# Three raw tiles of the down weights, two tiles for unrounded MLP units and one buffer for the plain quarters' parts, in a two-layer decoder trunk

## The chip, the cores and the metric

One core of one Trainium2 chip runs the whole program. The metric is device time in microseconds (us) of one launch; the time of a kernel is the median of several runs. A profile is taken of one further execution. The engines are TensorE (PE in the profile; PEld is its weight load), VectorE (DVE), ScalarE (ACT), GpSimd (POOL) and SyncE (SP); SP and POOL issue the DMAs that matter here.

## The reference

The kernel computes a trunk of two layers for 256 tokens of width 2048, in float32:

```
for l in range(2):
    h = rmsnorm(x, attn_norm_g[l]);  proj = h @ w_in[l]      # q | k | v | gate_b | gate_c | conv_in
    attn = differential attention of 8 heads (normed q and k, relative bias, subtracted softmaxes)
    conv = gate_b * causal_conv3(gate_c * conv_in)
    x = x + concat([attn, conv]) @ w_out[l]
    hm = rmsnorm(x, mlp_norm_g[l]) @ w_up[l]                 # 2048 -> 8192
    x = x + square(relu(hm)) @ w_down[l]                     # 8192 -> 2048
```

The change touches only the last two lines, the MLP.

## The kernel before

**Products.** TensorE works on float32 values that are rounded to a form it takes at full speed (F32R). So each operand is split into a high part (a rounded copy, made by ScalarE) and a low part (the value minus the high part, made by VectorE), and each product is three matmuls: high by high, high by low, low by high (TERMS, L48). What comes from weights goes raw by DMA into SBUF and is split there. For every 128x1024 stretch of weights this is one ScalarE copy of 1.06 us and one VectorE subtraction of 1.2 us.

**Up stage** (the loop at L999). The 8192 hidden units are made in 32 units of 256 (NP; i counts them). For each, two columns of up weights are multiplied (`up_part`, matmuls at L952, weights split at L818 and L819), evicted from PSUM (`evict`, ScalarE copy L962, VectorE add L963 into a tile `h`), and squared (`square`: relu L969, a factor per token L971, square L973, four sums L977 to L980). Then h is split into the parts of a tile f (L984, L985). Units of the list SEVEN are written unrounded to DRAM (L982); the others, but for the last two, as their two parts (L987).

Between the columns of unit i come the products of unit i − 2 (LAG) with the first 1024 columns of the down weights. A product of 2x2 blocks is done with seven block products in place of eight; so sums of the four quarters of the weights are wanted as well as the quarters themselves. `quarters` (L834) makes three jobs for a unit: `plain` loads the raw tile ("draw", L829, tag "draw" of the pool dpool) and splits one quarter into b1h and b1l, two into b2h and b2l (through `parts`, ScalarE L842, VectorE L843); `sums` makes the sums t (L856, L859, L860) and t13h, t13l; `more` makes t24h, t24l. The matmuls of the seven products stand at L995. The last two units, 30 and 31, have no sums and are multiplied in the ordinary way, eight block products each (`ordinary`, L1069, matmuls at L1077), after VectorE and ScalarE have begun to add the seven products into x (`seven_onto`, L1052, L1058, L1066).

**Down stage**, for the other 1024 columns. It begins with units 30 and 31 against whole columns (L1152). Then units 0 to 25 (27 in the second layer) are read back from DRAM, one unit ahead. `pair` (L1090 on) does this: a unit that is not in SEVEN comes back as its parts (tile "fb", L1097); a unit of SEVEN (2, 4, 7, 9 and so on) comes back unrounded into a tile "back" (L1101), which has the tag "h" and so shares the buffers of the up stage's h, and is split again (ScalarE L1102, VectorE L1103). Units of SEVEN are multiplied with `quarters` again, the others in the ordinary way. Blocks of four columns finish the stage.

**Order.** TensorE has its order written out by hand (`manual_schedule`). All weights pass one list of jobs (`Weights`); `take` hands the next to TensorE and has made the jobs up to three ahead of it (AHEAD). ScalarE, VectorE, POOL and SP are given their order by a scheduler, when the kernel is built; it places an instruction by its estimates once its inputs and its buffer are free, so an instruction of a later part of the program can come before one of an earlier part. Only instructions passed to `late` (L124) are kept in the order of the program. On the chip each engine then runs its instructions in that fixed order.

**Pools** (sizes for each partition): upool holds four raw tiles of 8 KB, fpool the tile h (4 KB, one buffer) and f (8 KB, two), dpool two raw tiles "draw" (8 KB), spool the quarters' parts: b1h and b1l (2 KB) and b2h and b2l (4 KB) with two buffers each, t, t13 and t24 with one.

Of the kernel before, what the change touches and what calls it, by code (L numbers as in the profile page):

```python
# [9 lines left out]
F32 = mybir.dt.float32  # L10
# [5 lines left out]
P = 128  # L16
# [12 lines left out]
CH = 512  # L29
# [76 lines left out]
def trunk(ctx: ExitStack, tc: tile.TileContext, x, w_in, w_out, conv_w, q_norm_g, k_norm_g,  # L106
# [19 lines left out]
    def bank(name):  # L126
        return ps.tile([P, CH], F32, tag="bank", name=name)
# [662 lines left out]
    def mlp(l, mnorm, last):  # L790
# [5 lines left out]
        with ExitStack() as scope:  # L796
            upool = scope.enter_context(tc.tile_pool(name="upool", bufs=4))
            fpool = scope.enter_context(tc.tile_pool(name="fpool", bufs=2))
            dpool = scope.enter_context(tc.tile_pool(name="dpool", bufs=2))
            spool = scope.enter_context(tc.tile_pool(name="spool", bufs=1))  # L800
            work.start(mnorm.factors(), 1)

# [2 lines left out]
            raws, forms = {}, {}  # L805
# [20 lines left out]
            def load_rows(i, col, pool=dpool, tag="draw"):  # L826
                raw = pool.tile([P, 2, 2 * CH], F32, tag=tag, name=tag)
                for k in range(2):
                    nc.sync.dma_start(  # L829
                        raw[:, k], w_down[l][(i * 2 + k) * P:(i * 2 + k + 1) * P,  # L830
                                             col:col + 2 * CH])
                return raw

            def quarters(i, col=0):  # L834


                keep = late if i == 0 or (i == SEVEN[0] and col) else lambda ins: None

                def parts(src, tag, bufs):
                    hi = spool.tile(list(src.shape), F32R, tag=f"{tag}h", name=f"{tag}h", bufs=bufs)  # L840
                    lo = spool.tile(list(src.shape), F32R, tag=f"{tag}l", name=f"{tag}l", bufs=bufs)
                    keep(nc.scalar.activation(hi, src, AF.Copy))  # L842
                    keep(nc.vector.tensor_sub(lo, src, hi.bitcast(F32)))  # L843
                    return hi, lo

                def plain():
                    raw = forms["raw"] = load_rows(i, col).rearrange("p k (n c) -> p k n c", n=2)
                    h1, l1 = parts(raw[:, 0, 0], "b1", 2)
                    h2, l2 = parts(raw[:, 1], "b2", 2)
                    return (h1, l1), (h2[:, 0], l2[:, 0]), (h2[:, 1], l2[:, 1])  # L850

                def sums():
                    raw = forms["raw"]
                    t = forms["t"] = spool.tile([P, 4, CH], F32, tag="t", name="t")

                    keep(nc.vector.tensor_sub(t[:, 0:2], raw[:, :, 1], raw[:, 0]))  # L856
                    h, lw = parts(t[:, 0:2], "t13", 1)

                    keep(nc.vector.tensor_add(t[:, 2], t[:, 1], raw[:, 0, 0]))  # L859
                    keep(nc.vector.tensor_sub(t[:, 3], raw[:, 1, 0], t[:, 2]))  # L860
                    return (h[:, 0], lw[:, 0]), (h[:, 1], lw[:, 1])

                def more():
                    h, lw = parts(forms["t"][:, 2:4], "t24", 1)
                    return (h[:, 0], lw[:, 0]), (h[:, 1], lw[:, 1])

                if (i, col) == (0, 0):
                    made = {}
                    forms["plain"] = lambda: made.update(p=plain())
                    forms["sums"] = lambda: made.update(s=sums())  # L870
                    return lambda: made["p"], lambda: made["s"], more
                return plain, sums, more
# [65 lines left out]
            def column_bank():  # L938
                acc = ps.tile([P, CH], F32, tag="av", name="upc", bufs=1)
                return acc.rearrange("p (h s) -> p h s", h=2)  # L940

            def up_part(acc, kh):

                hi, lo = weights.take()
                for part, wt in ((0, hi), (1, lo)):
                    for k in range(8):
                        a = mT[kh * 2 + k // KG]
                        while not a.ready:  # L950
                            work.tick()
                        nc.tensor.matmul(  # L952
                            acc[:, 0] if part else acc, wt[:, k],
                            a.ap[:, 0, k % KG] if part else a.ap[:, :, k % KG],
                            start=(part == 0 and kh == 0 and k == 0),
                            stop=(part == 1 and kh == 1 and k == 7), skip_group_check=True)
                        if k % 4 == 3:
                            work.tick()

            def evict(acc, dst):  # L960
                ev = nat.tile([P, 2, S], F32, tag="wide", name="ev")
                nc.scalar.activation(ev, acc, AF.Copy)  # L962
                nc.vector.tensor_add(dst.rearrange("p a c -> p (a c)"), ev[:, 0], ev[:, 1])  # L963
# [28 lines left out]
            def product(n, f, a, b, start, stop):  # L992

                for m, (pa, pw) in enumerate(TERMS):
                    nc.tensor.matmul(prods[n], f[:, pa, a], b[pw],  # L995
                                     start=(start and m == 0), stop=(stop and m == 2))

            fs = {}
            for i in range(NP):  # L999
                j = i - LAG  # L1000
                end = i == NP - 1
                h = fpool.tile([P, 8, P], F32, tag="h", name="h", bufs=1)
                if i == 0:
                    two = mm.tile([P, 2, CH], F32, tag="mm2", name="up0")
                    two = [two[:, c].rearrange("p (h s) -> p h s", h=2) for c in range(2)]
                    for kh in range(2):
                        for c in range(2):
                            up_part(two[c], kh)
                    forms["plain"]()
                    for c in range(2):  # L1010
                        evict(two[c], h[:, 2 * c:2 * c + 2])
                    fs[0] = square(0, h)
                    forms["sums"]()
                    continue
                for c in range(2):
                    if i < LAG:
                        acc = bank("upw").rearrange("p (h s) -> p h s", h=2)
                    else:
                        acc = column_bank()
                    up_part(acc, 0)  # L1020
                    up_part(acc, 1)
                    evict(acc, h[:, 2 * c:2 * c + 2])
                    if c == 1:
                        fs[i] = square(i, h)
                    if j == 0 and c == 0:
                        for pair in ((1, 6), (2, 3)):
                            w2 = mm.tile([P, 2, CH], F32, tag="mm2", name=f"pr{l}{pair[0]}")
                            prods[pair[0]], prods[pair[1]] = w2[:, 0], w2[:, 1]
                        for n in (5, 7, 4):
                            prods[n] = bank(f"pr{l}{n}")  # L1030
                    if j >= 0 and c == 0:
                        b11, b21, b22 = weights.take()
                        t1, t3 = weights.take()
                        f = fs[j]
                        product(1, f, A11, b11, j == 0, end)
                        product(2, f, A12, b21, j == 0, False)
                        product(3, f, S4, b22, j == 0, False)
                        product(5, f, S1, t1, j == 0, end)
                        work.tick()
                    elif j >= 0:  # L1040
                        t2, t4 = weights.take()
                        f = fs[j]
                        product(7, f, S3, t3, j == 0, end)
                        product(6, f, S2, t2, j == 0, end)
                        product(4, f, A22, t4, j == 0, False)
                        work.tick()
# [45 lines left out]
            def pair(i, f=None, at=0):  # L1092

                if f is None:
                    f = apool.tile([P, 2, 8, P], F32R, tag="a", name="fb")
                if i not in SEVEN:
                    nc.gpsimd.dma_start(  # L1097
                        f[:, :, at:at + 4].rearrange("p a k c -> p a (k c)"), hid[i])
                    return f
                back = fpool.tile([P, 8, P], F32, tag="h", name="back", bufs=1)  # L1100
                nc.gpsimd.dma_start(back.rearrange("p a c -> p (a c)"), hid7[i])  # L1101
                nc.scalar.activation(f[:, 0], back, AF.Copy)  # L1102
                nc.vector.tensor_sub(f[:, 1], back, f[:, 0].bitcast(F32))  # L1103
                return f
# [154 lines left out]
```

## Time and profile before

| What | Value |
| --- | --- |
| Median of 3 runs | 2139.8 us (2139.35 to 2141.16) |
| The profiled execution | 2141.08 us |
| Its span, first to last instruction | 2139.3 us |
| Mean granted TensorE clock | 1.000 |

The page of the profile gives busy times of the engines, the chain of work that ended last, and groups of instructions; the trace behind it gives each instruction's start and duration, the idle time before it and the instruction that ended that idle time. A row of the timeline has start, duration (us), engine, line, operation, the tiles it writes and reads, shape and count; in brackets stands the idle time of the engine before it and what it waited for. Rows with a count over 1 are several like instructions in a row, and the duration is that of all. A matmul of 128x512 is drawn 0.39 us long, but the next one starts 0.23 us after it; durations of neighbours overlap also on VectorE and ScalarE.

### The profile page before, as it was taken

What the parts mean: (1) busy time and instruction counts of PE and PEld (TensorE: products, weight loads), DVE (VectorE), ACT (ScalarE), POOL (GpSimd) and SP (SyncE); (2) the same over time, 40 slices, a digit from 0 to 9 for tenths busy, and PEclk for the clock granted to TensorE, in tenths of its full rate; (3) what the DMA queues carried; (4) which work ended last, traced back from release to release, by engine and by line L of the source; (5) the groups of instructions that cost most, each with busy time, mean ns of one, the idle gap of its engine ahead of it and who ended that gap; (6) DMA issues with size and microseconds to landing.
All of it is one profiled execution on the core that took longest, in us unless ns stands there. A gap on an engine that the chain in (4) does not pass through costs nothing.

```text
span 2139.3 us, 29295 instructions
## 1 busy us (share of the span) xinstructions
PE 2130.0 (100%) x10925; PEld 1817.7 (85%) x10925; DVE 1700.6 (79%) x2316; ACT 1317.1 (62%) x1776; POOL 164.4 (8%) x226
## 2 busy tenths in 40 slices
PE   9999999999999999999999999999999999999999
PEld 8888888888888888888888888888888888888887
DVE  6778655798888888798766786557988888888986
ACT  6666445666666666565565765456666666665653
POOL 3110200000000000011111101000000000000110
PEclk9999999999999999999999999999999999999999
DMA  8555766577777777789656558656877777777983
GB/s 271 178 164 168 253 188 186 187 247 228 230 236 227 233 233 226 239 302 307 226 168 178 165 161 264 187 177 200 250 231 223 241 231 223 240 226 251 315 309 128
DMA packets 298254, 476.01 MB, mean 223 GB/s; under 512 B 12707, under 2 KB 193781, under 8 KB 298112
## 3 DMA queue, kind: packets, MB, share of 16 engines
q1 hardware_dynamic: 269120, 406.76, 60.8%
q0 software_dynamic: 28800, 67.24, 9.3%
q8 instruction: 85, 1.39, 0.3%
q14 instruction: 57, 0.47, 0.1%
q10 hardware_dynamic: 192, 0.15, 0.0%
HBM read 440.52 MB, written 33.58 MB: 222 GB/s over the span
## 4 chain that ended last, share of the span: by engine, by line
PE 97%; DVE 1%; ACT 1%; DMA 1%; issue 0%; DVEq 0%; ACTq 0%
PE upc L952 31%; PE pr L995 13%; PE dn L1077 8%; PE o L386 8%; PE gb L408 4%; PE k L386 4%; PE q L386 4%; PE v L386 4%; PE ci L408 4%; PE gc L408 4%; PE dn L995 2%; PE dn L1152 2%; PE pr1r L995 1%; PE pr0r L995 1%; PE upw L952 1%; PE up L952 1%
## 5 line engine op out<-in xcount | busy, mean ns | idle before, releaser
L303 DVE TENSOR_TENSOR wlo<-raw,whi 128x1024 fp32r<-128x1024 f32 x274 | 341.6, 1248 | 222.6 <-ACT whi L302 221.2
L302 ACT ACTIVATE whi<-raw 128x1024 fp32r<-128x1024 f32 x274 | 290.4, 1060 | 306.5 <-PE o L386 73.6
L952 PE MATMUL upc<-nT,uhi 128*128 128x512 f32 x1920 | 477.8, 391 | 1.1 <-ACT ev L962 1.1
L818 ACT ACTIVATE uhi<-uraw 128x1024 fp32r<-128x1024 f32 x256 | 271.3, 1061 | 283.3 <-PE upc L952 262.5
L952 PEld LDWEIGHTS upc<-nT,uhi 128*128 128x128 f32 x1920 | 352.6, 188 | 70.0 <-ACT ev L962 1.9
L819 DVE TENSOR_TENSOR ulo<-uraw,uhi 128x1024 fp32r<-128x1024 f32 x256 | 312.6, 1222 | 111.1 <-ACT uhi L818 107.3
L952 PEld LDWEIGHTS upc<-nT,ulo 128*128 128x128 f32 x1920 | 261.9, 190 | 18.7
L952 PE MATMUL upc<-nT,ulo 128*128 128x256 f32 x1920 | 267.7, 282 | 0.0
L1077 PE MATMUL dn<-whi,fb 128*128 128x512 f32 x528 | 166.1, 389 | 0.0
L386 PE MATMUL o<-whi,cat 128*128 128x512 f32 x512 | 159.5, 390 | 0.0
L302 ACT ACTIVATE whi<-uraw 128x1024 fp32r<-128x1024 f32 x66 | 70.1, 1062 | 87.4 <-PE dn L1077 79.3
L1077 PEld LDWEIGHTS dn<-whi,fb 128*128 128x128 f32 x528 | 99.1, 188 | 20.5
L386 PEld LDWEIGHTS o<-whi,cat 128*128 128x128 f32 x512 | 96.2, 188 | 19.7
L842 ACT ACTIVATE b2h<-draw 128x1024 fp32r<-128x1024 f32 x81 | 85.7, 1059 | 29.8 <-PE pr L995 22.0
L843 DVE TENSOR_TENSOR t13l<-t,t13h 128x1024 fp32r<-128x1024 f32 x81 | 99.2, 1224 | 6.1 <-ACT t13h L842 3.7
L1077 PE MATMUL dn<-wlo,fb 128*128 128x512 f32 x264 | 102.7, 389 | 0.0
L843 DVE TENSOR_TENSOR b2l<-draw,b2h 128x1024 fp32r<-128x1024 f32 x81 | 98.6, 1218 | 3.2 <-ACT b2h L842 3.2
L843 DVE TENSOR_TENSOR t24l<-t,t24h 128x1024 fp32r<-128x1024 f32 x81 | 98.8, 1219 | 1.5 <-ACT t24h L842 0.3
L386 PE MATMUL o<-wlo,cat 128*128 128x512 f32 x256 | 99.6, 389 | 0.0
L856 DVE TENSOR_TENSOR t<-draw 128x1024 f32<-128x1024 f32 x81 | 98.7, 1219 | 0.5
L303 DVE TENSOR_TENSOR wlo<-uraw,whi 128x1024 fp32r<-128x1024 f32 x66 | 80.5, 1222 | 21.7 <-ACT whi L302 15.3
L995 PE MATMUL pr<-t13h,f 128*128 128x512 f32 x240 | 93.8, 391 | 0.0
(408 smaller groups left out, 4111.3 us busy)
## 6 DMA issues: line engine op xcount, KB each, us to landing
uraw<-in_w_up_dram SPq DMA_DIRECT2D x128, 1024.0 KB, 6.5
raw<-in_w_in_dram SPq DMA_DIRECT2D x191, 512.0 KB, 3.9
draw<-in_w_down_dram SPq DMA_DIRECT2D x170, 512.0 KB, 4.6
uraw<-in_w_down_dram SPq DMA_DIRECT2D x66, 512.0 KB, 5.1
raw<-in_w_out_dram SPq DMA_DIRECT2D x64, 512.0 KB, 3.6
hid0p<-f POOLq DMA_DIRECT2D x20, 512.0 KB, 6.6
raw<-in_w_down_dram SPq DMA_DIRECT2D x10, 1024.0 KB, 5.1
fb<-hid0p POOLq DMA_DIRECT2D x20, 512.0 KB, 6.7
```

Source lines behind the costliest of these rows:

```text
L302: pair = (nc.scalar.activation(hi, raw, AF.Copy), nc.vector.tensor_sub(lo, raw, hi.bitcast(F32)))
L303: nc.vector.tensor_sub(lo, raw, hi.bitcast(F32)))
L386: nc.tensor.matmul(acc[:, t], a.ap[:, pa, k % KG, t * P:(t + 1) * P], (hi, lo)[pw][:, j], start=(k == 0 and n == 0), stop=(k == nk - 1 and ...
L408: nc.tensor.matmul(acc[:, f, 0] if part else acc[:, f], wt[:, k % 4, fs], a.ap[:, 0, k % KG] if part else a.ap[:, :, k % KG], start=(part ...
L818: pair = (nc.scalar.activation(hi, src, AF.Copy), nc.vector.tensor_sub(lo, src, hi.bitcast(F32)))
L819: nc.vector.tensor_sub(lo, src, hi.bitcast(F32)))
L842: keep(nc.scalar.activation(hi, src, AF.Copy))
L843: keep(nc.vector.tensor_sub(lo, src, hi.bitcast(F32)))
L856: keep(nc.vector.tensor_sub(t[:, 0:2], raw[:, :, 1], raw[:, 0]))
L952: nc.tensor.matmul(acc[:, 0] if part else acc, wt[:, k], a.ap[:, 0, k % KG] if part else a.ap[:, :, k % KG], start=(part == 0 and kh == 0 ...
L995: nc.tensor.matmul(prods[n], f[:, pa, a], b[pw], start=(start and m == 0), stop=(stop and m == 2))
L1077: nc.tensor.matmul(prods[p], f[:, pa, 2 * k + t], b[pw][:, n], start=(p in starts and k == 0 and m == 0), stop=(stop and k == 1 and m == 2))
```

## The change

Three buffer counts are changed. The plain quarters' parts (b1h, b1l, b2h, b2l) have one buffer where they had two, which frees 12 KB of each partition. In this room go a third raw tile "draw" of the down weights (8 KB) and a second tile of the tag "h" (4 KB), for h in the up stage and for back in the down stage. Beside that, the raw tile and the sums are kept in a dictionary of each unit's own (`mine`) in place of the shared one (`forms`); this alone changes no instruction. TensorE's instructions and their order stay the same. The order of ScalarE, VectorE, POOL and SP is worked out anew by the scheduler. Line numbers of the changed kernel are higher by two from L840 on.

```diff
-            dpool = scope.enter_context(tc.tile_pool(name="dpool", bufs=2))
+            dpool = scope.enter_context(tc.tile_pool(name="dpool", bufs=3))
...
+                mine = {}
+
                 def parts(src, tag, bufs):
...
                 def plain():
-                    raw = forms["raw"] = load_rows(i, col).rearrange("p k (n c) -> p k n c", n=2)
-                    h1, l1 = parts(raw[:, 0, 0], "b1", 2)
-                    h2, l2 = parts(raw[:, 1], "b2", 2)
+                    raw = mine["raw"] = load_rows(i, col).rearrange("p k (n c) -> p k n c", n=2)
+                    h1, l1 = parts(raw[:, 0, 0], "b1", 1)
+                    h2, l2 = parts(raw[:, 1], "b2", 1)
                     return (h1, l1), (h2[:, 0], l2[:, 0]), (h2[:, 1], l2[:, 1])
 
                 def sums():
-                    raw = forms["raw"]
-                    t = forms["t"] = spool.tile([P, 4, CH], F32, tag="t", name="t")
+                    raw = mine["raw"]
+                    t = mine["t"] = spool.tile([P, 4, CH], F32, tag="t", name="t")
...
                 def more():
-                    h, lw = parts(forms["t"][:, 2:4], "t24", 1)
+                    h, lw = parts(mine["t"][:, 2:4], "t24", 1)
...
-                h = fpool.tile([P, 8, P], F32, tag="h", name="h", bufs=1)
+                h = fpool.tile([P, 8, P], F32, tag="h", name="h", bufs=2)
...
-                back = fpool.tile([P, 8, P], F32, tag="h", name="back", bufs=1)
+                back = fpool.tile([P, 8, P], F32, tag="h", name="back", bufs=2)
```

## The prediction

> **What bounds the kernel now.** I read the head of the page and its shares of busy time first, then the sums of the chain of waits.
>
> ```profile
> span 2139.3 us, 29295 instructions
> PE 2130.0 (100%) x10925; PEld 1817.7 (85%) x10925; DVE 1700.6 (79%) x2316; ACT 1317.1 (62%) x1776; POOL 164.4 (8%) x226
> PE 97%; DVE 1%; ACT 1%; DMA 1%; issue 0%; DVEq 0%; ACTq 0%
> ```
>
> TensorE is busy 2130.0 of 2139.3 us and is 97% of the chain that ended last. All its idle time is 9.3 us (0.4%); nothing that leaves TensorE's work as it is can win more, and the change leaves it so: its instruction order is the same in both kernels. So I ask two things only: which of the 9.3 us go, and whether a new wait comes. Next, the waits of TensorE, the two lines that stand in the MLP (waited for, us in total, times, longest):
>
> ```profile
> PE upc L952 <- ACT ev L962: 1.1, 1, 1.1
> PE pr L995 <- DVE f L985: 0.9, 2, 0.5
> ```
>
> Then the windows, one in the steady up stage (columns: us, PE, PEld, DVE, ACT, POOL busy with counts, granted clock, DMA share, GB/s):
>
> ```profile
> 530.00:694.00 164.00, 164.00 (x880) 141.93 (x879) 145.73 (x197) 109.82 (x135) 6.24 (x10) 1.00 0.74 230
> ```
>
> There TensorE has no gap at all, while VectorE is busy 145.73/164.00 = 89%. It keeps up, but an instruction that comes at the wrong place in its row is followed by others without a hole to catch up in. That is what I look for below.
>
> **What the change takes away.** Three stalls in each layer's MLP, or two and a trace, read from the timeline of ScalarE and TensorE (start, us, engine, line, operation; in brackets the idle time before and what ended it).
>
> ```profile
> 430.20 0.63 ACT L842 ACTIVATE b1h<-draw 128x512 fp32r<-128x512 f32 x1 [2.69 <-DMA draw<-in_w_down_dram]
> 431.68 0.58 ACT L962 ACTIVATE ev<-upc 128x512 f32<-128x512 f32 x1
> 430.80 0.39 PE L995 MATMUL pr<-t24h,f 128*128 128x512 f32 x1
> 432.31 0.96 PE L952 MATMUL upc<-nT,uhi 128*128 128x512 f32 x3 [1.13 <-ACT ev L962]
> ...
> 470.11 0.40 PE L995 MATMUL pr<-b1l,f 128*128 128x512 f32 x1
> 470.97 0.50 PE L995 MATMUL pr<-b1h,f 128*128 128x512 f32 x1 [0.47 <-DVE f L985]
> ...
> 911.34 0.61 PE L1152 MATMUL dn<-whi,f 128*128 128x512 f32 x2
> 912.02 0.50 PE L1152 MATMUL dn<-wlo,f 128*128 128x512 f32 x1
> ...
> 1973.53 0.61 PE L1152 MATMUL dn<-whi,f 128*128 128x512 f32 x2
> 1974.21 0.50 PE L1152 MATMUL dn<-wlo,f 128*128 128x512 f32 x1
> ...
> 895.25 0.39 PE L1077 MATMUL pr<-whi,f 128*128 128x512 f32 x1
> 900.46 0.61 PE L1077 MATMUL pr<-whi,f 128*128 128x512 f32 x2
> ```
>
> From 895.25 to 900.46 are 23 matmuls without a stall, 5.21/23 = 0.227 us from start to start; what a start is later than that is a stall.
>
> (1) 432.31 − 430.80 − 0.23 = 1.28 us, first layer only: ScalarE stands 2.69 us at b1h until its raw tile has landed, and the eviction of upc, which could have run, stands behind it. A third raw tile lets that load go a pair earlier: gone. (2) 470.97 − 470.11 − 0.23 = 0.63 us, and by the waits' "0.9, 2" once more in the other layer: the low half of f is late because the one unrounded tile h is held. With a second h the chain of the next pair starts at once: gone, 1.26 us. (3) 912.02 − 911.34 − 2 × 0.227 = 0.23 us, and 1974.21 − 1973.53 − 2 × 0.227 = 0.23 in the other layer, a low part of the first columns of the down stage; VectorE's order there is rearranged, and I let it go in both layers: 0.46 us. Sum **−3.0 us** at most. Each restart also shows a slower first matmul (0.50 for 0.39), five times 0.11 = 0.55 in all, which I leave to the range.
>
> **What costs nothing: one b1 and one b2.** No instruction is added. In the order of the changed kernel these parts are written, as before, right behind the product that frees them; the trace of before already shows such a write waiting for the product:
>
> ```profile
> 616.28 1.06 ACT L842 ACTIVATE b2h<-draw 128x1024 fp32r<-128x1024 f32 x1 [0.43 <-PE pr L995]
> 629.94 0.40 PE L995 MATMUL pr<-b1h,f 128*128 128x512 f32 x1
> ```
>
> The next product that reads such a part starts 629.94 − 616.28 = 13.66 us after that write began. All four parts take some 3.6 us (the b1h row 0.63, b2h 1.06, and their low parts, by the 128x512 and 128x1024 subtracts shown below, 0.68 + 1.23). So TensorE's other matmuls hide it; without that cover it would be up to 3.6 us for each of some 30 quartered units a layer, and the cover would have to shrink by 10 us first. In the down stage it is thinner: at least one ordinary unit of 24 matmuls (24 × 0.227 = 5.4 us) stands between two quartered ones, beside the rest of the quartered unit's own matmuls. Still over 3.6. I take 0.
>
> **What is added: the junction of the up and the down stage.** In the changed kernel the second h buffer is free when the first rounded unit is read back for the down stage ("back", L1103 in the new numbering), and a raw tile is too. The written-out order of each engine (ScalarE and VectorE, which the scheduler arranges) then has that unit's work *ahead of* the last pair's chain. Of the changed kernel, in order; "+" is what stood behind the last f before:
>
> ```
> ScalarE: + fb copy | ev | e | + t13h | relu | whi | + whi (L302, waits for the end of unit 30) | square | f copy
> VectorE: wlo | + fb sub | + t | add | e x e x e | + t13l | + t | ratio | x | + wlo | + x | + x | + wlo | + t | f sub
> ```
>
> The last unit's (31's) matmuls come right behind unit 30's on TensorE (that begin at 895.25, above):
>
> ```profile
> 901.14 0.61 PE L1077 MATMUL pr<-whi,f 128*128 128x512 f32 x2
> ```
>
> Unit 30 takes 24 matmuls, 895.25 to 900.69; unit 31 begins at 900.69 with the high half of f, and its third matmul, 901.14, reads the low half. Before, both were just in time:
>
> ```profile
> 893.52 1.23 DVE L303 TENSOR_TENSOR wlo<-draw,whi 128x1024 fp32r<-128x1024 f32 x1 [1.57 <-ACT whi L302]
> 894.66 0.42 DVE L963 TENSOR_TENSOR h<-ev 128x256 f32<-128x256 f32 x1
> ...
> 896.76 0.42 DVE L971 TENSOR_TENSOR h<-h,ratiob 128x256 f32<-128x256 f32 x1
> 897.09 0.74 DVE L1050 SCALAR_TENSOR_TENSOR e<-pr,rowf,e 128x512 f32<-128x512 f32 x1
> 897.75 0.74 DVE L1050 SCALAR_TENSOR_TENSOR x<-pr,rowf,x 128x512 f32<-128x512 f32 x1
> ...
> 899.67 0.68 DVE L985 TENSOR_TENSOR f<-h,f 128x512 fp32r<-128x512 f32 x1
> 900.27 1.28 DVE L1066 TENSOR_TENSOR x<-x,e 128x512 f32<-128x512 f32 x2
> ...
> 907.83 1.21 DVE L1103 TENSOR_TENSOR fb<-back,fb 128x1024 fp32r<-128x1024 f32 x1
> 908.96 1.21 DVE L856 TENSOR_TENSOR t<-draw 128x1024 f32<-128x1024 f32 x1
> ```
>
> f sub ended at 900.35, 0.79 us before it was needed. Now 18 instructions run from the wlo of 893.52 to f sub. Start to start, from these rows: 128x1024 subtract 894.66 − 893.52 = 1.14; 128x256 897.09 − 896.76 = 0.33; 128x512 with a scalar 897.75 − 897.09 = 0.66; 128x512 plain 900.27 − 899.67 = 0.60. Six of 1.14 (wlo, fb sub, t, t13l, wlo, wlo), two of 0.33 (add, ratio), four of 0.66 (three e, one x), six of 0.60 (four x, two t): 6.84 + 0.66 + 2.64 + 3.60 = 13.74. f sub starts at 893.52 + 13.74 = 907.26, ends at 907.94, and TensorE, which in the rows above goes on 0.05 us after such an end (470.97 after 469.70 + 1.22), starts its third matmul at 907.99: **907.99 − 901.14 = 6.85 us late**.
>
> No input is later than that sum has it, so VectorE has no hole in it; I checked the ones from ScalarE:
>
> ```profile
> 893.39 0.59 ACT L962 ACTIVATE ev<-upc 128x512 f32<-128x512 f32 x1
> 897.21 0.63 ACT L973 ACTIVATE h<-h 128x512 f32<-128x512 f32 x1 [1.23 <-DVE h L971]
> 900.89 1.06 ACT L302 ACTIVATE whi<-raw 128x1024 fp32r<-128x1024 f32 x1 [1.43 <-PE pr L1077]
> 904.58 1.04 ACT L1102 ACTIVATE fb<-back 128x1024 fp32r<-128x1024 f32 x1
> ```
>
> With the fb copy ahead, ev comes about 1 us later, at 894.4, before its add at 896.9. ScalarE then stands at the whi until unit 30 ends (900.89), and its square needs the ratio, now at 893.52 + 8.73 = 902.25 to 902.67 (11 of the 18 instructions ahead of it). Square and copy follow by 0.6 us each: the high half of f is there near 904.0. So TensorE idles about 3.2 us at the first matmul of unit 31, does two, and idles again about 3.5 us at the third. No row of before shows this wait itself. Its bounds: below, 3.2 us if only ScalarE's share told; above, some 8 if the read-back landed late. That load is issued once the last but one f is rounded, and loads of that queue and size (512 KB) took 6.7 us:
>
> ```profile
> 883.61 0.69 DVE L985 TENSOR_TENSOR f<-h,f 128x512 fp32r<-128x512 f32 x1
> fb<-hid0p POOLq DMA_DIRECT2D x20, 512.0 KB, 6.7
> ```
>
> 883.61 + 0.69 + 6.7 = 891.0, 2.4 us ahead of 893.4; if it took half as long again (10.0 us) it would be 0.9 late, and all behind it: 7.8. I take 6.85, by the row. Behind the last unit nothing more is late: the extra work that VectorE did early (fb sub, t, t13l, at 907.83 and after before) is then done. SP's and POOL's queues only get the draw and back loads earlier, and both have room.
>
> In the second layer the order is the same and so are the distances:
>
> ```profile
> 1955.71 1.23 DVE L303 TENSOR_TENSOR wlo<-draw,whi 128x1024 fp32r<-128x1024 f32 x1 [1.57 <-ACT whi L302]
> ...
> 1963.33 0.62 PE L1077 MATMUL pr<-whi,f 128*128 128x512 f32 x2
> ```
>
> 1955.71 + 13.74 + 0.73 − 1963.33 = 6.85 again. **Sum: 2 × 6.85 − 3.0 = +10.7 us.** The profiled execution took 2141.08 (span 2139.3 and 1.8 around it), so it would take 2151.8. That is 1.3 above the median of 2139.8, from which I go: **2150.5 us**, 0.5% slower.
>
> [...]
>
> **The rivals.** *Clock*: TensorE drops to half speed in the new idle time. The trace has a granted clock of 1.00 in the window above, and no idle time over 1.13 us in the MLP, so it can't show it; at its start it shows slow matmuls:
>
> ```profile
> 1.05 5.06 PE L160 MATMUL warm<-ones 128*128 128x128 f32 x22 [1.05 <-DVE mhalf L152]
> 7.02 0.83 PE L160 MATMUL warm<-ones 128*128 128x128 f32 x6
> ```
>
> 5.06/22 = 0.23 each, later 0.83/6 = 0.14 (ends included): about 5 us at half speed, so 2.5 lost. Twice that is +5.0: 2155.5. For it: two idle stretches of 3.2 and 3.5 us almost joined. Against: each is short, and two matmuls lie between. [...]
>
> *The other side: no stall.* If ScalarE or VectorE could start a ready instruction ahead of one that waits, the last chain (relu, square, f) would not stand behind the read-back, and only the gain stayed: 2139.8 − 3.0 = 2136.8, within 0.2%. It decides when the chain loses less than the 0.79 us of its margin. Against it: the eviction of 431.68 stood behind b1h.
>
> *Half of it*: VectorE finds its row shorter than I count, and only ScalarE's wait tells: 2 × 3.2 − 3.0 = +3.4, 2143.2, within 0.2%.
>
> *One b1 and b2 do hold TensorE*: a further wait in each of some 30 units a layer; already 0.5 us each is +30, to 2180. For it: VectorE at 89%. Against it: 13.7 us of room.
>
> **How the numbers follow.** Forecast 0.64; clock 0.17; no stall 0.06; half 0.06; b1 and b2 0.04; faster by more than I found 0.03. 0.2% is 4.3 us, about what a measurement of this kernel can tell from no change: forecast, clock and b1/b2 are slower, 0.85; no stall and half are within, 0.12; faster 0.03. The range runs from 2146 (the gain larger by the restarts and the sum short by 2 us a layer) to 2157 (late read-back or clock in both layers).
>
> **What would show it.** Right: on TensorE two new waits of about 3 us in each layer, for ScalarE's f and then VectorE's f, behind unit 30's last matmul; the waits of 1.1 for ev and of 0.9 for f gone; ScalarE's fb copy ahead of the last ev; steady windows as full as before. Wrong: f sub ending before unit 30 does; repeated waits for b1 or b2 parts; a granted clock below 1.00 behind the junction (the clock rival).

## The result and the profile after

The changed kernel took 2154.8 us (median of 5 runs, 2152.9 to 2156.9), the kernel before 2141.2 us (5 runs, 2139.4 to 2141.9): a ratio of 1.0068, 95% interval 1.0057 to 1.0080. The forecast was 2150.5 us with a range of 2146 to 2157. So the direction and the range held, and the value was 4 us short. The five runs differ in how much the clock of TensorE was lowered: from the shortest to the longest, their mean granted clocks are 0.997, 0.997, 0.996, 0.996 and 0.995. The profiled execution (2153.07 us) is the second shortest.

The page of the changed kernel, its clock by core, and TensorE's waits (waited for, us in total, times, longest):

```profile
span 2151.2 us, 29237 instructions
PE 2132.1 (99%) x10925; PEld 1819.5 (85%) x10925; DVE 1706.8 (79%) x2316; ACT 1330.4 (62%) x1776; POOL 164.1 (8%) x226
```

```profile
core 0: 2151.2 us, clock 0.997
```

```profile
PE pr L1079 <- DVE f L987: 6.5, 2, 3.2
PE pr L1079 <- ACT f L986: 6.4, 2, 3.2
```

These two lines are the two new waits that the prediction described, once in each layer. The waits of 1.1 for ev and of 0.9 for f are no longer in the list. TensorE's busy time is 2.1 us longer for the same 10925 matmuls, and its mean granted clock is 0.997 in place of 1.000; the forecast had nothing for that. The timeline of TensorE at the junction of the first layer, and the restarts in the second:

```profile
896.45 0.39 PE L1079 MATMUL pr<-whi,f 128*128 128x512 f32 x1
900.03 0.50 PE L1079 MATMUL pr<-whi,f 128*128 128x512 f32 x1 [3.19 <-ACT f L986]
...
903.99 1.22 PE L1079 MATMUL pr<-whi,f 128*128 128x512 f32 x2 [3.23 <-DVE f L987]
905.00 0.63 PE L1079 MATMUL pr<-wlo,f 128*128 128x512 f32 x1
905.43 1.06 PE L1079 MATMUL pr<-whi,f 128*128 128x512 f32 x2
...
911.45 0.39 PE L1154 MATMUL dn<-whi,f 128*128 128x512 f32 x1
...
1969.82 0.50 PE L1079 MATMUL pr<-whi,f 128*128 128x512 f32 x1 [3.19 <-ACT f L986]
1973.78 1.22 PE L1079 MATMUL pr<-whi,f 128*128 128x512 f32 x2 [3.23 <-DVE f L987]
...
1980.58 0.39 PE L1154 MATMUL dn<-whi,f 128*128 128x512 f32 x1
```

Unit 30 ends with the matmul of 896.45, so unit 31 could begin at 896.68 and its third matmul at 897.13. It begins at 900.03, and the third starts at 903.99, which is 6.86 us late. From then on the matmuls start 0.43 us apart in place of 0.227 (905.00 to 905.43), for some 5 us. From unit 31's third matmul to the first of the next stage are 22 steps. In the kernel before they took 4.99 us, from 901.14 to this row:

```profile
906.13 0.39 PE L1152 MATMUL dn<-whi,f 128*128 128x512 f32 x1
```

Now they take 911.45 − 903.99 = 7.46 us in the first layer and 1980.58 − 1973.78 = 6.80 us in the second: 2.47 and 1.81 us more, together 4.3 us.

VectorE and ScalarE there, in the new order:

```profile
889.51 1.23 DVE L303 TENSOR_TENSOR wlo<-draw,whi 128x1024 fp32r<-128x1024 f32 x1 [1.57 <-ACT whi L302]
890.65 1.22 DVE L1105 TENSOR_TENSOR fb<-back,fb 128x1024 fp32r<-128x1024 f32 x1
...
898.23 0.42 DVE L973 TENSOR_TENSOR h<-h,ratiob 128x256 f32<-128x256 f32 x1
...
903.24 0.69 DVE L987 TENSOR_TENSOR f<-h,f 128x512 fp32r<-128x512 f32 x1
```

```profile
889.38 1.04 ACT L1104 ACTIVATE fb<-back 128x1024 fp32r<-128x1024 f32 x1
890.33 0.58 ACT L964 ACTIVATE ev<-upc 128x512 f32<-128x512 f32 x1
...
898.68 0.63 ACT L975 ACTIVATE h<-h 128x512 f32<-128x512 f32 x1 [0.70 <-DVE h L973]
899.34 0.63 ACT L986 ACTIVATE f<-h 128x512 fp32r<-128x512 f32 x1
```

From the wlo to f sub are 903.24 − 889.51 = 13.73 us, with no hole between (13.74 was worked out). The read-back's fb comes ahead of the last eviction on both engines, and the high half of f is done at 899.97, 0.06 us before TensorE goes on.

In the steady up stage TensorE has no gap, as before (columns as in the prediction's window):

```profile
530.00:694.00 164.00, 164.00 (x875) 141.64 (x874) 146.67 (x198) 112.92 (x135) 6.23 (x10) 1.00 0.75 230
```

### The profile page after: what moved, and what is told of

The parts are those of the page before. It is cut to its first block, busy times and chain, and to the rows that moved or that the text cites. A ratio compares the mean times of both kernels' runs of the same rounds, so it can differ in the third digit from the quotient of the medians.

```text
span 2151.2 us, 29237 instructions
## 1 busy us (share of the span) xinstructions
PE 2132.1 (99%) x10925; PEld 1819.5 (85%) x10925; DVE 1706.8 (79%) x2316; ACT 1330.4 (62%) x1776; POOL 164.1 (8%) x226
## 4 chain that ended last, share of the span: by engine, by line
PE 97%; DVE 1%; ACT 1%; issue 0%; DMA 0%; SPq 0%; DVEq 0%; ACTq 0%
PE upc L954 31%; PE pr L997 13%; PE dn L1079 8%; PE o L386 8%; PE ci L408 4%; PE gb L408 4%; PE k L386 4%; PE v L386 4%; PE q L386 4%; PE gc L408 4%; PE dn L1154 2%; PE dn L997 2%; PE pr1r L997 1%; PE pr0r L997 1%; PE upw L954 1%; PE up L954 1%
## 5 line engine op out<-in xcount | busy, mean ns | idle before, releaser
L844 ACT ACTIVATE t24h<-t 128x1024 fp32r<-128x1024 f32 x81 | 85.1, 1051 | 13.0 <-DVE t L862 6.8
```

## The experiments

The theory: the second buffer of the tag h lets the read-back of the down stage's first unrounded unit go ahead of the last pair's chain, and TensorE waits for it; then its clock falls. The rivals: the time is lost to the single b1 and b2, or to the third raw tile; or the slow matmuls have another cause. Each experiment gives its median and that of the kernel before, measured along with it on the same chip. The interval behind a ratio is that of 95%.

**One h** (third raw tile kept).

```diff
-                h = fpool.tile([P, 8, P], F32, tag="h", name="h", bufs=2)
+                h = fpool.tile([P, 8, P], F32, tag="h", name="h", bufs=1)
...
-                back = fpool.tile([P, 8, P], F32, tag="h", name="back", bufs=2)
+                back = fpool.tile([P, 8, P], F32, tag="h", name="back", bufs=1)
```

> The changed kernel with one buffer for the tag h again (h and back), everything else as changed. My theory (the second h lets the read-back go ahead of the last pair's chain): the order at the junction is that of before, both waits for unit 31's f and the slow matmuls behind them are gone, the wait of 432.31 stays gone, the waits for f of 0.63 each are back: 1.3 to 2.2 us faster than before. Rival (one b1 and b2, or the third raw tile, costs the time): still slower than before, by up to 13 us.

2136.5 us against 2140.2, ratio 0.9984 (0.9975 to 0.9992): 3.7 us faster than before. The waits for unit 31's f are gone, so the second h is needed for the loss. But the expectation was wrong on one point: the wait for f of 0.63 us did not come back. Nothing in the MLP stands in its list of TensorE's waits, only two lines that before had too:

```profile
PE sc L604 <- DVE cat L682: 1.2, 2, 0.6
PE warm L160 <- DVE mhalf L152: 1.1, 1, 1.1
```

**Two raw tiles** (second h kept).

```diff
-            dpool = scope.enter_context(tc.tile_pool(name="dpool", bufs=3))
+            dpool = scope.enter_context(tc.tile_pool(name="dpool", bufs=2))
```

> The changed kernel with two raw tiles of the down weights again, so the second h alone remains (b1 and b2 have one buffer). The read-back's copy and subtraction and one t still stand ahead of the last chain, but t13l, two t and one wlo no longer. Sum ahead of f sub: 4 x 1.14 + 2 x 0.33 + 4 x 0.66 + 4 x 0.60 = 10.3 us in place of 13.7, so one wait, at the third matmul of unit 31, of about 3.3 us a layer, and none at its first. With the 2.1 us that the second h wins: 4.6 us slower than before. If a single idle stretch of 3.1 us also lowers the clock: up to 4 more, 8 to 9 slower. Rival (the third raw tile brings the loss): no slower than before.

2150.3 us against 2140.2, ratio 1.0043 (1.0031 to 1.0056): slower with one raw tile fewer too. The 10.1 us between the medians are more than the 4.6 without the clock and more than the 8 to 9 with it. TensorE at the junction, and the row of VectorE that explains the size of the wait:

```profile
901.81 0.91 PE L1079 MATMUL pr<-whi,f 128*128 128x512 f32 x2 [3.80 <-DVE f L987]
902.52 0.63 PE L1079 MATMUL pr<-wlo,f 128*128 128x512 f32 x1
```

```profile
896.99 1.23 DVE L858 TENSOR_TENSOR t<-draw 128x1024 f32<-128x1024 f32 x1 [0.50 <-DMA draw<-in_w_down_dram]
```

One wait, at the third matmul, as worked out; it is 0.5 us longer because the one t ahead of f waits for its raw tile. The next matmuls start 0.43 us apart again, and the mean granted clock is 0.998, with 0.97 from 880 to 930 us: the clock fell behind a single idle stretch of 3.8 us. The third raw tile makes the loss larger (it lets t13l and another t go ahead too), but without the second h it does no harm, as the run with one h showed.

**The last chain first**: all buffers as changed, but the order of the scheduler corrected at two places. A list `ends` holds the last pair's two f instructions; `behind` queues what is traced within it behind these, or behind the splits of the last block (`weights.pairs[-5]`), by the scheduler's `issue_after`.

```diff
+                def job():
+                    with behind(i, col, weights.pairs[-5:][0] if weights.pairs else None):
+                        return sums()
+                return plain, job, more
...
-                nc.scalar.activation(f[:, 0], back, AF.Copy)
-                nc.vector.tensor_sub(f[:, 1], back, f[:, 0].bitcast(F32))
+                with behind(i, 1):
+                    nc.scalar.activation(f[:, 0], back, AF.Copy)
+                    nc.vector.tensor_sub(f[:, 1], back, f[:, 0].bitcast(F32))
```

> The changed kernel with all its buffers, but the read-back's copy and subtraction queued behind the last pair's f, and the sums t of that first unit behind the splits of the last block of whole columns. My theory: the waits for unit 31's f go, nothing takes their place, and what the buffers win stays: 3.0 to 3.7 us faster than before. Rival (the buffers cost elsewhere): slower than that, at or above before.

2135.6 us against 2140.2, ratio 0.9980 (0.9971 to 0.9989): 4.5 us faster than before, where 3.0 to 3.7 were expected, and the lowest median of all. The same buffers with fb behind f lose nothing, so the order was the cause:

```profile
896.77 0.68 DVE L999 TENSOR_TENSOR f<-h,f 128x512 fp32r<-128x512 f32 x1
...
899.72 1.22 DVE L1118 TENSOR_TENSOR fb<-back,fb 128x1024 fp32r<-128x1024 f32 x1
```

**Filled waits**: the changed kernel, in which TensorE adds products with a tile of zeros while it would wait, 13 of 128x512 ahead of unit 31 and 13 ahead of its third matmul. They leave the sums as they are. A padding tile in SBUF is made smaller by what the tile of zeros takes.

```diff
+    zero = const.tile([P, 32], F32R, tag="zero", name="zero")
+    nc.scalar.activation(zero, ones[:, :32], AF.Copy, scale=0.0)
...
+            def nothing(n, rhs):
+                for _ in range(n):
+                    nc.tensor.matmul(prods[2][:32], zero, rhs, start=False, stop=False)
...
+                    if stop and k == 0:
+                        nothing(13, b[0][:, 0])
...
+                            if stop and k == 0 and n == t == 0 and m == 2:
+                                nothing(13, b[0][:, 0])
```

> The changed kernel, same order on ScalarE and VectorE at the junction, but TensorE multiplies by zeros in its waits: 13 matmuls (3.0 us) ahead of the first matmul of unit 31 and 13 ahead of its third. Theory (the 0.43 us matmuls behind the second wait are the clock, lowered by the idle time): granted clock 1.00, matmuls at 0.227 throughout, 4 us faster than the profile of the changed kernel and some 4 to 6 faster than its median: 8 to 10 us slower than before. Rival (they are slow because of something else that happens there, such as the burst of loads): the same time as the changed kernel, with the slow matmuls still there.

2150.0 us against 2140.2, ratio 1.0046 (1.0033 to 1.0058): 9.8 us slower than before, where 8 to 10 were expected. TensorE, first layer:

```profile
897.25 3.17 PE L1076 MATMUL pr<-whi,zero 128*32 128x512 f32 x13
900.60 0.50 PE L1089 MATMUL pr<-whi,f 128*128 128x512 f32 x1 [0.18 <-ACT f L988]
...
901.17 3.15 PE L1076 MATMUL pr<-whi,zero 128*32 128x512 f32 x13
904.55 0.73 PE L1089 MATMUL pr<-whi,f 128*128 128x512 f32 x2 [0.23 <-DVE f L989]
905.12 0.40 PE L1089 MATMUL pr<-wlo,f 128*128 128x512 f32 x1
```

f is as late as without the filling: unit 31 could begin at 897.25 and does at 900.60, 3.35 us later, as in the changed kernel (896.68 and 900.03). But behind it two steps take 905.12 − 904.55 = 0.57 us, the restart's 0.11 among them, where they took 1.01 us (903.99 to 905.00), and the mean granted clock is 1.000 (from 880 to 930 us 1.00, where it was 0.93). From 880 to 930 us the DMA engines are as busy in both (a share of 0.60 and 0.62), so the loads do not explain it. So the slow matmuls were the clock, which fell with the waits left idle and did not with them filled. Its price is 4.7 us by the ratios (1.0068 − 1.0046 = 0.0022), and 3.8 by the distances of the medians (13.7 and 9.8). In the profiles it is 4.0: the 22 steps behind the second wait take 5.15 and 5.14 us here, 7.46 and 6.80 in the changed kernel.

**One b1 and b2 alone**: the kernel before with this one part.

```diff
-                    h1, l1 = parts(raw[:, 0, 0], "b1", 2)
-                    h2, l2 = parts(raw[:, 1], "b2", 2)
+                    h1, l1 = parts(raw[:, 0, 0], "b1", 1)
+                    h2, l2 = parts(raw[:, 1], "b2", 1)
```

> The kernel before with one buffer for b1 and b2, and nothing else changed: two raw tiles, one h, 12 KB left unused. My prediction priced this part at 0 and gave the wins at 432.31 and 470.97 to the third raw tile and the second h. But both runs that undo one of these have kept both wins, so the theory now: b1h can't be written early any more, so it no longer stands ahead of the evictions on ScalarE; the wins belong to this part: 2.5 to 3.7 us faster than before. Rival (either of the two extra buffers is enough for the wins): as before, within 0.5 us.

2136.5 us against 2140.0, ratio 0.9983 (0.9974 to 0.9992): 3.5 us faster. It has the wins of steps (1) and (2) without any extra buffer. ScalarE and TensorE at the place of the 1.28 us wait, and TensorE at that of the 0.63 us wait:

```profile
428.58 1.04 ACT L984 ACTIVATE f<-h 128x1024 fp32r<-128x1024 f32 x1
429.53 0.58 ACT L962 ACTIVATE ev<-upc 128x512 f32<-128x512 f32 x1
```

```profile
430.21 0.39 PE L995 MATMUL pr<-t24h,f 128*128 128x512 f32 x1
430.43 1.75 PE L952 MATMUL upc<-nT,uhi 128*128 128x512 f32 x7
...
468.09 0.40 PE L995 MATMUL pr<-b1l,f 128*128 128x512 f32 x1
468.33 0.39 PE L995 MATMUL pr<-b1h,f 128*128 128x512 f32 x1
```

ev follows f at once where b1h stood between before (430.20, ahead of ev at 431.68). With two buffers the scheduler could place b1h as soon as its estimates had the raw tile there, ahead of the evictions; with one it must place it behind the product that frees the buffer. In the kernel before, ScalarE waits for the raw tile at b1h six times (waited for, us, times, longest); in the runs with one b1 and b2 it never does:

```profile
ACT b1h L842 <- DMA draw<-in_w_down_dram: 8.8, 6, 2.7
```

Two of these six times belong to the 0.63 us waits, one in each layer. In the first layer of the kernel before, the square of the pair (L973) had its input at 457.13, but stood behind b1h and b2h, which waited for their raw tile; the low half of f came at 469.70, late for TensorE:

```profile
456.89 0.63 ACT L842 ACTIVATE b1h<-draw 128x512 fp32r<-128x512 f32 x1 [1.58 <-DMA draw<-in_w_down_dram]
458.13 1.06 ACT L842 ACTIVATE b2h<-draw 128x1024 fp32r<-128x1024 f32 x1 [0.61 <-DMA draw<-in_w_down_dram]
...
460.04 0.62 ACT L973 ACTIVATE h<-h 128x512 f32<-128x512 f32 x1
469.70 1.22 DVE L985 TENSOR_TENSOR f<-h,f 128x1024 fp32r<-128x1024 f32 x1
```

With one b1 and b2:

```profile
455.44 0.64 ACT L973 ACTIVATE h<-h 128x512 f32<-128x512 f32 x1 [0.18 <-DVE h L971]
462.01 1.22 DVE L985 TENSOR_TENSOR f<-h,f 128x1024 fp32r<-128x1024 f32 x1 [0.22 <-ACT f L984]
```

Counted from the matmul with b1l (470.11 before, 468.09 here), the square is 2.6 us earlier and the low half of f 5.7 us; what is beyond the 2.6 comes from the order behind the square.

**One b1 and b2, sums later**: the same, with the sums t of the first quartered unit of the down stage behind the last block's splits.

```diff
+                def job():
+                    with behind(i, col):
+                        return sums()
+                return plain, job, more
```

> The kernel before with one buffer for b1 and b2, and the sums t of the first quartered unit of the down stage queued behind the splits of the last block of whole columns (as in the version with the last chain first, but with two raw tiles and one h). Theory: it takes back the 0.33 us a layer at 912.02 as well and is level with the version that has all buffers and the last chain first, 3.0 to 4.5 us faster than before: the two extra buffers are then worth nothing. Rival (a third raw tile or a second h wins something of its own): slower than that version by 1 us or more.

2137.3 us against 2140.0, ratio 0.9985 (0.9976 to 0.9994): 2.7 us faster than before, less than the 3.0 to 4.5 expected, and 0.8 us behind the run without the later sums. Its one profile has no stall at the place of 912.02 any more, and its span of 2134.8 is 0.6 shorter, so the trace does not show why the median is higher. It isn't settled whether the two extra buffers are worth something, with the last chain first: that version is 1.7 us ahead of this one and 0.9 ahead of the single b1 and b2. The first of these is what the rival asked for (1 us or more), but the intervals of the ratios overlap.

**Part of the idle time left**: two versions of the filled waits, one with the second wait left open, one with 6 matmuls of zeros in each.

```diff
-                            if stop and k == 0 and n == t == 0 and m == 2:
-                                nothing(13, b[0][:, 0])
```

> As the version that multiplies by zeros in both waits, but only ahead of the first matmul of unit 31; one idle stretch of 3.2 us is left at the third, in each layer. [...] If a stretch that is mostly idle is enough, as the idle 3.8 us with slow matmuls 0.7 us after their end suggest: matmuls of 0.43 us in some executions, 1 to 5 us slower than the filled version, and a wide spread of times.

2153.6 us against 2140.0, ratio 1.0063 (1.0050 to 1.0076): 3.6 us more than with both filled, and a mean granted clock of 0.998 in all five runs. From 880 to 930 us the clock is 0.97, and from 1945 to 1995 the same: it fell behind a single idle stretch of 3.2 us in each layer:

```profile
904.51 0.73 PE L1087 MATMUL pr<-whi,f 128*128 128x512 f32 x2 [3.22 <-DVE f L989]
...
905.31 1.00 PE L1087 MATMUL pr<-whi,f 128*128 128x512 f32 x2
906.10 0.63 PE L1087 MATMUL pr<-wlo,f 128*128 128x512 f32 x1
```

```diff
-                        nothing(13, b[0][:, 0])
+                        nothing(6, b[0][:, 0])
...
-                                nothing(13, b[0][:, 0])
+                                nothing(6, b[0][:, 0])
```

> As the version that multiplies by zeros in both waits, but with 6 such matmuls (1.4 us) in each in place of 13: two idle stretches of about 1.8 us remain in each layer, with 1.4 to 1.8 us of work between them. If only long idle stretches count: clock 1.00, 9.8 us slower than before. [...]

2151.0 us against 2140.0, ratio 1.0051 (1.0038 to 1.0064): 1.0 us more than with both filled. The first layer and the second differ:

```profile
900.71 0.50 PE L1089 MATMUL pr<-whi,f 128*128 128x512 f32 x1 [1.79 <-ACT f L988]
...
901.28 2.66 PE L1076 MATMUL pr<-whi,zero 128*32 128x512 f32 x6
...
1969.81 0.50 PE L1089 MATMUL pr<-whi,f 128*128 128x512 f32 x1 [1.80 <-ACT f L988]
1970.38 1.55 PE L1076 MATMUL pr<-whi,zero 128*32 128x512 f32 x6
```

After the same idle 1.8 us the six matmuls take 2.66 us in the first layer and 1.55 in the second. The granted clock is 0.93 from 880 to 930 us and 1.00 from 1945 to 1995: it fell behind one idle stretch of 1.8 us and not behind the other. In two of the five runs the mean granted clock is 1.000, in three 0.998.

## Why the prediction was right in direction and short in size

- **The junction**: right, to 0.01 us. Predicted 6.85 us late in each layer by 18 counted instructions, 13.74 us; measured 6.86 and 13.73. The idle stretches of 3.19 and 3.23 us are the 3.2 and 3.5 of the working, the second a little shorter. The run with the last chain first shows that this order, with the clock that it lowers, is the whole loss.
- **The clock**: the step that failed. It stood as a rival with a chance of 0.17 and "each is short, and two matmuls lie between" against it; the sum left it out. It came in both layers: 4.3 us in the profile (4.0 without the slower restarts) and 3.8 to 4.7 us by the filled waits, where +5.0 was priced. With it the sum is 10.7 + 4.3 = 15.0, against 13.7 measured between the medians and 14.6 by the ratio. The two profiles lie only 11.9 us apart. There the stretches around the junctions add 9.0 and 8.3 us, the stalls that went in the up stage give back 3.1, and places that the change does not touch are 2.4 us shorter.
- **What the change takes away**: the size was right, the owner wrong, so that the size came out was luck. The waits of 1.28 and 2 × 0.63 us went, with their slower restarts (and one of 0.2 us in the second layer that the prediction did not count). But step (1) gave the first to the third raw tile and step (2) the others to the second h, and "one b1 and one b2" stood at 0. The single b1 and b2 alone wins 3.5 us, and each run that lacked one of the two other parts kept these wins. No run has a third raw tile or a second h without the single b1 and b2, so whether they would have done it too stays open. I took the buffer that a wait names for the one that helps, and didn't ask what sets the order of the instructions that stood in the way (b1h ahead of ev, b1h and b2h ahead of the square).
- **The down stage's wlo** (0.23 us a layer): gone, as forecast; also gone in the run with the last chain first, and still there with one h.
- **No cost in steady state for one b1 and b2**: right. TensorE is busy 164.00 of 164.00 us in the same window.
- **The other side** (engines that pass a waiting instruction) and **half of it**: neither came. f's low half had its inputs at 899.97 and ran at 903.24, behind what stood ahead of it in VectorE's row, and that row was as long as counted. In the kernel before, ScalarE idled 0.61 us in front of b2h (458.13) with the square ready.
- Executions differ in places that the change does not touch. A matmul of the first layer's mixer (ci, which waits for whi) waits 1.0 us in the profile of the kernel before, 0.6 with one b1 and b2, 0.5 with the last chain first, and is in no list of the changed kernel; the first 22 matmuls of the program take 5.06 us before and 4.33 in the changed kernel. Differences of 1 us and less between versions are therefore left open here.

## What to carry to other kernels

Where a scheduler writes the order, a freed buffer is also a licence to run ahead: read, at each junction of stages, what the new order puts in front of the chain that the busiest engine waits for, and count it in start-to-start times; the same buffers with the order corrected were 4.5 us faster instead of 13.7 slower. Fewer buffers can help for the same reason: one b1 and b2 kept a copy from standing, with its wait for a DMA, ahead of an eviction or a square. Where a change lets TensorE idle, look whether its granted clock fell behind the wait, and add that to the price: here, behind idle stretches of 3.19 and 3.23 us at each of the two junctions, 2.5 and 1.8 us.

## What the runs showed of the hardware that was not expected

The kernel before shows no fall of the granted clock in its MLP: TensorE idles there for 1.13 us at most, and the clock is 1.00. In these runs it fell behind idle stretches of 3.2 us and more in both layers (3.19 and 3.23 us in the changed kernel, 3.80 and 3.63 with two raw tiles, 3.2 with only the first wait filled), and behind 1.8 us in one layer of two with 6 matmuls of zeros in each wait. The slow time did not always begin at the restart. With only the first wait filled, three matmuls take 0.80 us from the restart to the start of the fourth (904.51 to 905.31), and only behind these do the starts come 0.43 us apart (906.10, 906.53). In the version with two raw tiles the first slow one starts 0.7 us after the restart (901.81, 902.52). The record of the granted clock in the trace of the changed kernel has it at half around the third matmul of unit 31, first layer and second (columns as in the prediction's window; the granted clock is the 1.00 or 0.50 ahead of the last two numbers):

```profile
900.03:902.15 2.12, 0.73 (x2) 0.29 (x2) 2.12 (x4) 0.00 (x0) 0.00 (x0) 1.00 0.39 54
902.15:908.97 6.82, 4.99 (x12) 3.97 (x13) 5.61 (x7) 1.37 (x2) 0.54 (x1) 0.50 0.59 214
908.97:911.45 2.48, 2.48 (x13) 2.00 (x11) 1.70 (x2) 0.75 (x1) 0.00 (x0) 1.00 0.00 0
...
1969.82:1970.52 0.70, 0.70 (x2) 0.30 (x2) 0.70 (x2) 0.00 (x0) 0.00 (x0) 1.00 0.00 0
1970.52:1977.34 6.82, 3.59 (x9) 2.81 (x9) 6.23 (x8) 1.06 (x1) 0.54 (x1) 0.50 0.70 231
1977.34:1980.58 3.24, 3.24 (x15) 2.63 (x14) 2.28 (x4) 1.06 (x1) 0.00 (x0) 1.00 0.01 5
```

In the first layer the clock is at half from 902.15 to 908.97, in the second from 1970.52 to 1977.34, 6.82 us each time. The third matmul starts 903.99 − 902.15 = 1.84 us behind the fall in the first layer and 1973.78 − 1970.52 = 3.26 us behind it in the second, where less of the work came into the slow time. Half of TensorE's busy time in it, 4.99/2 = 2.5 us and 3.59/2 = 1.8 us, is what the 22 steps took more (2.47 and 1.81 us). What amount of idle time brings a fall, and what sets its moment and its length, was not shown.
